# A hybrid convolution-attention block: the convolution's running sum moved to PSUM, the attention scores to shared one-bank halves

## The chip, the cores and the metric

One core of one Trainium2 chip runs the whole kernel. The metric is the device time of one execution in microseconds (us), from the first to the last instruction with the little that lies around them. Engines are named as in the profile: PE is TensorE's matmul, PEld its weight load, DVE VectorE, ACT ScalarE, POOL GpSimd, SP the engine that issues the DMAs. PSUM has eight banks of 512 fp32 values on each of 128 partitions.

## The reference

The input `x` has 2048 rows of 1024 channels. The block is

```
h    = rmsnorm(x)
proj = h @ w_in                       # 7680 columns: glu a, glu b, conv gate, q, k, v, attention gate, two merge gates
c    = silu(layernorm(depthwise_conv31(a * sigmoid(b)) + bias))     # causal, 31 taps, one filter per channel
y_c  = (c * silu(conv_gate)) @ w_conv_out
att  = attention(rope(q), rope(k), v) # 16 query heads, 4 key/value heads, window 128, one sink per head
y_a  = (att * silu(attn_gate)) @ w_attn_out
out  = rmsnorm(x + (sigmoid(m_c) * y_c + sigmoid(m_a) * y_a) @ w_out)
```

Two pieces matter here. The convolution is, for each of 1024 channels, a sum over 31 taps `w[j] * u[t + j - 30]`, then a bias. The attention takes blocks of 128 queries; each block sees its own 128 keys and the 128 before, and the softmax has a sink term beside the scores.

## The kernel before, in words

The 2048 rows are worked in two sweeps of 1024 (`sweep(s)`). In a sweep the channels lie on partitions, in eight chunks of 128, and the rows lie along the free axis, so a tile of the convolution is 128 x 1024. Each product is made from three fp32r matmuls (high times high, high times low, low times high); a projection of 128 columns is two halves of 24 matmuls of 128 x 512, into one of three one-bank tiles of the pool `mm_ps` (line 281).

The order of a sweep is: the projections of k, v and q with rope, interleaved with the eight chunks of the gated unit (`glu_items`), then the four gate projections (`ag`, `cg`, `ma`, `mc`), while convolution and attention run beside them; then the two branch outputs (`ya`, `yc`) and the output product (line 877). In the first sweep the low parts of the weights are made on POOL (`wlo`, line 242) and stored; in the second they are loaded.

PE's order is written out by a planner, the class `Line`. It adds up an estimate of PE's time and inserts steps of other work between groups of three matmuls when their due time has come. Attention on one block of one key/value head is three such steps: the scores (line 566), 22 us later on the planner's clock the transposes of the probabilities (`tpp`, line 594), 16 us later the product with the values (`ov`, line 614). A new block starts each 13.8 us (`ATT_EVERY`), 32 blocks in a sweep. The convolution's taps, one DVE instruction each on 128 x 1024, are handed out every 2.4 us of the planner's clock (`CONV_EVERY`). The other engines' rows are put in order by the compiler's scheduler; each engine then executes its own list strictly in that order and waits at an instruction whose inputs or output buffer are not ready.

The convolution of chunk `c`: the first tap (line 389) multiplies and adds the bias and writes `cv`, a tile in SBUF; 30 more (line 393) each read `glu` at an offset and `cv`, and write `cv`. After the last tap POOL adds `cv` to `csum` for the layer norm.

PSUM's eight banks go to `mm_ps` (three), `tp_ps` (three one-bank tiles, taken in turn) and `sc_ps` (one tile of two banks). All scores of a block, four heads by 256 keys, go to the `sc` tile: ACT copies the older half of the keys to `sb` in SBUF (line 573), DVE lays the block's own keys over it where the mask allows (line 574), and with that both banks are free. From `tp_ps` come `tpp`, which is read by an ACT cast to `pt` (line 599) and a DVE subtraction for its low part (line 242 with `pt<-tpp`), and `ov`, which is read by two ACT copies and two DVE additions (lines 617 and 618). After `pt`, POOL makes `pc`, the part of it that the causal edge lets through (line 605).

Of the kernel before, what the change touches and what calls it, by code (L numbers as in the profile page):

```python
# [12 lines left out]
F32 = mybir.dt.float32  # L13
F32R = mybir.dt.float32r
I32 = mybir.dt.int32
AF = mybir.ActivationFunctionType
ALU = mybir.AluOpType
AX = mybir.AxisListType

P = 128  # L20
# [3 lines left out]
T = 1024  # L24
# [3 lines left out]
TAPS = 31  # L28
# [4 lines left out]
GQ = NH // NKV  # L33
# [20 lines left out]
def hybrid_block(ctx: ExitStack, tc: tile.TileContext, x, par_d, w_in, w_conv, sinks, w_attn, w_out,  # L54
                 fin_g, rope_t, out):
    nc = tc.nc
    pe, act, dve, pool = nc.tensor, nc.scalar, nc.vector, nc.gpsimd
# [4 lines left out]
    work = ctx.enter_context(tc.tile_pool(name="work", bufs=2))  # L62
    mm_ps = ctx.enter_context(tc.tile_pool(name="mm_ps", bufs=3, space=bass.MemoryType.PSUM))
    tp_ps = ctx.enter_context(tc.tile_pool(name="tp_ps", bufs=3, space=bass.MemoryType.PSUM))
    sc_ps = ctx.enter_context(tc.tile_pool(name="sc_ps", bufs=1, space=bass.MemoryType.PSUM))
    dram = ctx.enter_context(tc.tile_pool(name="dram", bufs=1, space=bass.MemoryType.DRAM))

    x2, out2 = x[0], out[0]
# [8 lines left out]
    C = [f"c{i}" for i in range(8)]  # L77
# [3 lines left out]
    def slot(tag, shape, dt, name):  # L81
        n = int(np.prod(shape[1:]))
        full = HALO + T + 2 if tag in WIDE else 1024
        t = slots.tile([P, full], dt, tag=tag, name=name)
        v = t[:, 0:n]
        if len(shape) == 3:
            v = v.rearrange("p (a b) -> p a b", b=shape[2])
        elif len(shape) == 4:
            v = v.rearrange("p (a b c) -> p a b c", b=shape[2], c=shape[3])
        return v  # L90
# [6 lines left out]
    def next_of(key, tags):  # L97
        rot.setdefault(key, cycle(range(len(tags))))
        return tags[next(rot[key])]


    def load_first(half):
        xs = []
        for j in range(4):
# [17 lines left out]
    causal = const.tile([P, P], F32, name="causal")  # L122
    dve.memset(causal, 1.0)
    pool.affine_select(out=causal, in_=causal, pattern=[[-1, P]], compare_op=ALU.is_ge, fill=0.0,
                       base=0, channel_multiplier=1)
    causal_i = causal.bitcast(I32).unsqueeze(1).broadcast_to([P, GQ, P])
    eps = const.tile([P, 2], F32, name="eps_t")
    dve.memset(eps, EPS)
    act.activation(out=eps[:, 1:2], in_=eps[:, 0:1], func=AF.Sqrt)
# [8 lines left out]
    def tap(c, j):  # L138
        return par[:, c, j:j + 1]
# [3 lines left out]
    def cbias(c):  # L143
        return par[:, c, TAPS + 1:TAPS + 2]
# [96 lines left out]
    def split_lo(out_, full, hi, eng):  # L241
        eng.tensor_tensor(out=out_, in0=full, in1=f(hi), op=ALU.subtract)  # L242
# [129 lines left out]
    def sweep(s):  # L372
# [4 lines left out]
            return hT[half][k]  # L377

        glu_slot = [C[7], C[6], AT[14], C[7], C[6], AT[14], C[7], AT[14]]
        glu, cv, conv_done = {}, {}, []  # L380
        csum = work.tile([P, T], F32, tag="ln0", name=f"csum{s}", bufs=1)


        def conv_ops(c):
            ops = []

            def first():
                cv[c] = slot(C[c], [P, T], F32, f"cv{s}_{c}")
                dve.tensor_scalar(out=cv[c], in0=glu[c][:, 0:T], scalar1=tap(c, 0), scalar2=cbias(c),
                                  op0=ALU.mult, op1=ALU.add)  # L390

            def nxt(j):
                dve.scalar_tensor_tensor(out=cv[c], in0=glu[c][:, j:j + T], scalar=tap(c, j),  # L393
                                         in1=cv[c], op0=ALU.mult, op1=ALU.add)
                if j == TAPS - 1:
                    if not conv_done:
                        pool.tensor_copy(out=csum, in_=cv[c])
                    else:
                        pool.tensor_tensor(out=csum, in0=csum, in1=cv[c], op=ALU.add)
                    conv_done.append(c)  # L400
                    if len(conv_done) == KC:
                        line.start(ln_chain())

            ops.append(first)
            for j in range(1, TAPS):
                ops.append(lambda j=j: nxt(j))
            return ops
# [143 lines left out]
        def attention(n):  # L551
            g, b = divmod(n, NB)
            begun.add(n)
            u = f"{s}_{g}_{b}"
            blk = s * NB + b
            first = blk == 0
            q, k = qk.pop(n)
            load_qk(n + 1)
            sc = sc_ps.tile([P, GQ, 2, P], F32, tag="sc", name=f"sc{u}")
            for h in range(GQ):  # L560
                for j in range(2):
                    if first:
                        o, r = sc[:, h, 1, :], k[:, j, P:]
                    else:
                        o, r = sc[:, h], k[:, j]
                    pe.matmul(out=o, lhsT=q[:, h, :], rhs=r, start=(j == 0), stop=(j == 1))  # L566
            ss = slot(next_of("ss", AT[4:7] + AT[13:14]), [P, 1024], F32, f"ss{u}")
            sb = ss[:, 0:512].rearrange("p (h q) -> p h q", q=P)
            oT, ga = (ss[:, c:c + 256].rearrange("p (a q) -> p a q", q=P) for c in (512, 768))
            if first:  # L570
                pool.memset(sb, NEG)
            else:
                act.copy(sb, sc[:, :, 0, :])
            dve.copy_predicated(out=sb, mask=causal_i, data=sc[:, :, 1, :])
            st = work.tile([P, 6, GQ], F32, tag="st", name=f"st{u}", bufs=4)
            mx, ngm, es, den, rinv, dlt = (st[:, i, :] for i in range(6))
            hd = slice(g * GQ, (g + 1) * GQ)
            dve.tensor_reduce(out=mx, in_=sb, axis=AX.X, op=ALU.max, negate=True)
            dve.scalar_tensor_tensor(out=ngm, in0=mx, scalar=SCALE, in1=nsink[:, hd], op0=ALU.mult,  # L579
                                     op1=ALU.min)  # L580
            dve.tensor_tensor(out=dlt, in0=sink_bc[:, hd], in1=ngm, op=ALU.add)
            act.activation(out=es, in_=dlt, func=AF.Exp)
            for h in range(GQ):
                act.activation(out=sb[:, h, :], in_=sb[:, h, :], func=AF.Exp, scale=SCALE,  # L584
                               bias=ngm[:, h:h + 1], accum_out=den[:, h:h + 1])
            dve.tensor_tensor(out=den, in0=den, in1=es, op=ALU.add)
            dve.reciprocal(out=rinv, in_=den)
            for h in range(GQ):
                act.activation(out=sb[:, h, :], in_=sb[:, h, :], func=AF.Copy, scale=rinv[:, h:h + 1])
            yield 0.96, LAT[0]  # L590

            tpp = tp_ps.tile([P, GQ, P], F32, tag="tp", name=f"tpp{u}")
            for h in range(GQ):
                pe.transpose(out=tpp[:, h, :], in_=sb[:, h, :], identity=ident)  # L594
            e2 = slice(s * KC + 2 * g, s * KC + 2 * g + 2)
            qs = slice(b * P, (b + 1) * P)
            nc.sync.dma_start(out=ga, in_=spill["ag"][e2, :, qs].rearrange("c p q -> p c q"))
            pt = slot(next_of("pt", AT[7:9]), [P, 2, GQ, P], F32R, f"pt{u}")
            act.copy(pt[:, 0], tpp)
            split_lo(pt[:, 1], tpp, pt[:, 0], dve)  # L600
            if first:
                seq = [(v_of(g, b), pt)]
            else:
                pc = slot(next_of("pc", AT[9:11]), [P, 2, GQ, P], F32R, f"pc{u}")
                pool.affine_select(out=pc, in_=f(pt), pattern=[[0, 2], [0, GQ], [1, P]],  # L605
                                   compare_op=ALU.is_ge, fill=0.0, base=0, channel_multiplier=-1)
                seq = [(v_of(g, b - 1), pt), (vd[b // 2][:, b % 2, g, :], pc)]
            yield 0.44, LAT[1]

            ov = tp_ps.tile([P, GQ, P], F32, tag="tp", name=f"ov{u}")  # L610
            nm = 2 * len(seq)
            for i in range(nm):
                vv, pp = seq[i // 2]
                pe.matmul(out=ov, lhsT=vv, rhs=pp[:, i % 2], start=(i == 0), stop=(i == nm - 1))  # L614
            ovp = ov.rearrange("p (i r) q -> p i r q", r=2)
            for r, own, other in ((0, slice(0, HD), slice(HD, P)), (1, slice(HD, P), slice(0, HD))):
                act.copy(oT[own], ovp[other, :, r, :])
                dve.tensor_tensor(out=oT[own], in0=ovp[own, :, r, :], in1=oT[own], op=ALU.add)
            dve.tensor_tensor(out=oT, in0=oT, in1=ga, op=ALU.mult)
            hl = sb.rearrange("p (l c) q -> p l c q", c=2)  # L620
            act.copy(hl[:, 0].bitcast(F32R), oT)
            split_lo(hl[:, 1].bitcast(F32R), oT, hl[:, 0], dve)
            for i in range(2):
                nc.sync.dma_start(out=d_a[e2, :, i, qs].rearrange("c p q -> p c q"), in_=hl[:, i])
            done[n] = True
            if n == NKV * NB - 1 and s + 1 < NSWEEP:
                pool.tensor_copy(out=v_halo, in_=f(vt[NB // 2 - 1][:, 1]).rearrange(
                    "p g (a d) -> p g a d", d=HD))
            yield nm * MM_US, 0.0
# [327 lines left out]
```

## Time and profile before

| | |
|---|---|
| runs | 2091.12, 2091.15, 2089.14 us; median 2091.12 |
| profiled execution | span 2089.1 us, as long as the shortest run |
| PE busy | 2046.8 us, 98% of the span |
| PEld, DVE, ACT, POOL busy | 1674.2, 1395.1, 1014.5, 478.3 us |
| mean granted TensorE clock | 0.993 of full |

A row of the profile names line, engine, operation, output and inputs; times in it are us unless marked ns. "Idle before, releaser" is how long an engine stood still before an instruction, and what let it go. PE is pipelined, so its busy share says little about how fast it runs: its waits and its granted clock say more.

### The profile page before, as it was taken

To read this page: it belongs to the slowest core of one execution; us is meant where nothing else is said; L and a number is where in the kernel's file an instruction comes from. 1 tells how busy PE (TensorE), PEld (TensorE's weight loads), DVE (VectorE), ACT (ScalarE), POOL (GpSimd) and SP (SyncE) were. 2 spreads that over 40 slices of the span, in tenths; PEclk is the share of its full clock that TensorE was granted. 3 is DMA by queue.
4 is the path that set the end of the run, shared out by engine and by line. 5 is a ranking of instruction groups with operands and counts; after the bars stand their busy time and mean duration, and the time that the engine had idled before them with its cause. 6 is when DMAs were issued, how large, how long until landed. Compare 5 with 4: busy or idle time off the path is not lost.

```text
span 2089.1 us, 27438 instructions
## 1 busy us (share of the span) xinstructions
PE 2046.8 (98%) x9256; PEld 1674.2 (80%) x9256; DVE 1395.1 (67%) x1901; ACT 1014.5 (49%) x2253; POOL 478.3 (23%) x336
## 2 busy tenths in 40 slices
PE   7999999999999999999999999999999999999998
PEld 6787888787787878888888888888888888888887
DVE  4979779899888348123559596698888934341324
ACT  6221376665666646122442214767777674621222
POOL 2445433343333322243001131121111110000200
PEclk9999999999999999999999999999999999999999
DMA  7444645554445875646344456555655577574432
GB/s 250 134 143 149 191 148 154 165 158 148 152 146 178 262 238 190 203 141 222 101 151 132 141 162 202 173 158 175 174 163 165 174 228 257 166 232 146 139 120 81
DMA packets 265819, 355.89 MB, mean 170 GB/s; under 512 B 28112, under 2 KB 126544, under 8 KB 265680
## 3 DMA queue, kind: packets, MB, share of 16 engines
q1 hardware_dynamic: 265680, 354.16, 53.2%
q8 instruction: 73, 1.20, 0.2%
q14 instruction: 66, 0.54, 0.1%
HBM read 234.51 MB, written 119.54 MB: 169 GB/s over the span
## 4 chain that ended last, share of the span: by engine, by line
PE 80%; DVE 5%; issue 2%; ACT 1%; DMA 0%; POOL 0%; SPq 0%; DVEq 0%; ACTq 0%; POOLq 0%
PE mm_ag L281 9%; PE o L877 8%; PE mm_mc L281 8%; PE mm_yc L281 8%; PE mm_ya L281 8%; PE mm_cg L281 7%; PE mm_gb L281 6%; PE mm_ma L281 6%; PE mm_ga L281 6%; DVE cv L393 3%; PE mm_q_b L281 2%; PE sc L566 2%; PE ov L614 2%; PE mm_q_a L281 2%; PE tpp L594 1%
## 5 line engine op out<-in xcount | busy, mean ns | idle before, releaser
L393 DVE SCALAR_TENSOR_TENSOR cv<-glu,par,cv 128x1024 f32<-128x1024 f32 x480 | 680.5, 1418 | 6.2
L605 POOL TENSOR_SCALAR_AFFINE_SELECT pc<-pt 128x1024 fp32r<-128x1024 f32 x60 | 101.9, 1698 | 458.0 <-DVE pt L242 390.4
L877 PE MATMUL o<-wo,mT 128*128 128x512 f32 x768 | 181.3, 394 | 0.0
L281 PE MATMUL mm_cg<-hT,whi_cg 128*128 128x512 f32 x512 | 164.2, 402 | 5.2 <-ACT glu L415 3.3
L877 PEld LDWEIGHTS o<-wo,mT 128*128 128x128 f32 x768 | 143.1, 188 | 32.1
L281 PE MATMUL mm_ga<-hT,whi_ga 128*128 128x512 f32 x512 | 162.4, 398 | 3.0 <-ACT ag L434 2.8
L281 PE MATMUL mm_ma<-hT,whi_ma 128*128 128x512 f32 x512 | 161.2, 396 | 1.0 <-ACT ma L434 1.0
L281 PE MATMUL mm_ag<-hT,whi_ag 128*128 128x512 f32 x512 | 160.9, 395 | 1.2 <-ACT glu L415 1.2
L281 PE MATMUL mm_gb<-hT,whi_gb 128*128 128x512 f32 x512 | 161.9, 398 | 0.0
L281 PE MATMUL mm_mc<-hT,whi_mc 128*128 128x512 f32 x512 | 159.8, 393 | 0.0
L281 PE MATMUL mm_yc<-uT,whi_yc 128*128 128x512 f32 x512 | 159.4, 392 | 0.0
L281 PE MATMUL mm_ya<-aT,whi_ya 128*128 128x512 f32 x512 | 158.7, 391 | 0.0
L281 PEld LDWEIGHTS mm_cg<-hT,whi_cg 128*128 128x128 f32 x512 | 95.8, 192 | 25.9 <-ACT glu L415 3.7
L281 PEld LDWEIGHTS mm_ga<-hT,whi_ga 128*128 128x128 f32 x512 | 95.1, 190 | 24.4 <-ACT ag L434 3.2
L281 PEld LDWEIGHTS mm_yc<-uT,whi_yc 128*128 128x128 f32 x512 | 96.2, 188 | 21.8
L281 PEld LDWEIGHTS mm_mc<-hT,whi_mc 128*128 128x128 f32 x512 | 96.0, 188 | 21.9 <-ACT mc L434 0.2
L281 PEld LDWEIGHTS mm_ya<-aT,whi_ya 128*128 128x128 f32 x512 | 96.1, 188 | 21.0
L281 PEld LDWEIGHTS mm_gb<-hT,whi_gb 128*128 128x128 f32 x512 | 95.5, 190 | 20.2
L281 PEld LDWEIGHTS mm_ag<-hT,whi_ag 128*128 128x128 f32 x512 | 94.2, 188 | 21.1 <-ACT glu L415 1.7
L281 PEld LDWEIGHTS mm_ma<-hT,whi_ma 128*128 128x128 f32 x512 | 94.0, 188 | 20.9 <-ACT ma L434 1.8
L584 ACT ACTIVATE ss<-ss,st 128x128 f32<-128x128 f32 x256 | 99.8, 391 | 20.2 <-DVE st L579 19.5
L815 POOL TENSOR_TENSOR lmc<-lmc,mp 128x512 f32<-128x512 f32 x32 | 41.9, 1310 | 275.5 <-DVE lmc L814 271.2
(363 smaller groups left out, 4338.6 us busy)
## 6 DMA issues: line engine op xcount, KB each, us to landing
qk<-d_q SPq DMA_DIRECT2D x256, 64.0 KB, 2.6
d_a<-ss SPq DMA_DIRECT2D x128, 128.0 KB, 1.9
aT<-d_a SPq DMA_DIRECT2D x32, 512.0 KB, 6.1
qk<-d_k SPq DMA_DIRECT2D x240, 64.0 KB, 2.1
raw_gb<-in_w_in_dram SPq DMA_DIRECT2D x34, 256.0 KB, 3.8
raw_ga<-in_w_in_dram SPq DMA_DIRECT2D x34, 256.0 KB, 3.4
raw_ag<-in_w_in_dram SPq DMA_DIRECT2D x32, 256.0 KB, 3.8
d_ag<-ag SPq DMA_DIRECT2D x32, 256.0 KB, 2.2
```

The source lines that it names most:

```text
L281: pe.matmul(out=ps, lhsT=a, rhs=b, start=(k == 0 and i == 0), stop=(k == KC - 1 and i == 2))
L393: dve.scalar_tensor_tensor(out=cv[c], in0=glu[c][:, j:j + T], scalar=tap(c, j), in1=cv[c], op0=ALU.mult, op1=ALU.add)
L566: pe.matmul(out=o, lhsT=q[:, h, :], rhs=r, start=(j == 0), stop=(j == 1))
L584: act.activation(out=sb[:, h, :], in_=sb[:, h, :], func=AF.Exp, scale=SCALE, bias=ngm[:, h:h + 1], accum_out=den[:, h:h + 1])
L594: pe.transpose(out=tpp[:, h, :], in_=sb[:, h, :], identity=ident)
L605: pool.affine_select(out=pc, in_=f(pt), pattern=[[0, 2], [0, GQ], [1, P]], compare_op=ALU.is_ge, fill=0.0, base=0, channel_multiplier=-1)
L614: pe.matmul(out=ov, lhsT=vv, rhs=pp[:, i % 2], start=(i == 0), stop=(i == nm - 1))
L815: pool.tensor_tensor(out=g, in0=g, in1=mp[e][:, half * TH:(half + 1) * TH], op=ALU.add)
L877: pe.matmul(out=ps, lhsT=a[:, c0:c0 + P], rhs=r, start=(k == 0 and i == 0), stop=(k == KC - 1 and i == 2))
```

## The change

The pool `sc_ps` is gone, and its two banks become `cv_ps`, one tile of 128 x 1024 fp32 for the convolution's running sum (`acc`). The first tap writes `acc`, the next 29 read and write it, and the last reads `acc` and writes `cv` in SBUF, which is only taken then. The scores now come in two tiles of one bank each, two heads in each, from `tp_ps`, so that a block takes four tiles in turn from its three banks: two for scores, one for `tpp`, one for `ov`. ACT's copy and DVE's masked copy are made once for each half.

```
-    sc_ps = ctx.enter_context(tc.tile_pool(name="sc_ps", bufs=1, space=bass.MemoryType.PSUM))
+    cv_ps = ctx.enter_context(tc.tile_pool(name="cv_ps", bufs=1, space=bass.MemoryType.PSUM))
...
             def first():
-                cv[c] = slot(C[c], [P, T], F32, f"cv{s}_{c}")
-                dve.tensor_scalar(out=cv[c], in0=glu[c][:, 0:T], scalar1=tap(c, 0), scalar2=cbias(c),
+                acc[c] = cv_ps.tile([P, T], F32, tag="acc", name=f"acc{s}_{c}")
+                dve.tensor_scalar(out=acc[c], in0=glu[c][:, 0:T], scalar1=tap(c, 0), scalar2=cbias(c),
                                   op0=ALU.mult, op1=ALU.add)
             def nxt(j):
-                dve.scalar_tensor_tensor(out=cv[c], in0=glu[c][:, j:j + T], scalar=tap(c, j),
-                                         in1=cv[c], op0=ALU.mult, op1=ALU.add)
+                to = acc[c]
+                if j == TAPS - 1:
+                    to = cv[c] = slot(C[c], [P, T], F32, f"cv{s}_{c}")
+                dve.scalar_tensor_tensor(out=to, in0=glu[c][:, j:j + T], scalar=tap(c, j),
+                                         in1=acc[c], op0=ALU.mult, op1=ALU.add)
...
-            sc = sc_ps.tile([P, GQ, 2, P], F32, tag="sc", name=f"sc{u}")
+            scs = []
             for h in range(GQ):
+                if h % 2 == 0:
+                    scs.append(tp_ps.tile([P, 2, 2, P], F32, tag="tp", name=f"sc{u}_{h // 2}"))
+                sc = scs[-1][:, h % 2]
...
-            else:
-                act.copy(sb, sc[:, :, 0, :])
-            dve.copy_predicated(out=sb, mask=causal_i, data=sc[:, :, 1, :])
+            for i, sc in enumerate(scs):
+                part = sb[:, 2 * i:2 * i + 2, :]
+                if not first:
+                    act.copy(part, sc[:, :, 0, :])
+                dve.copy_predicated(out=part, mask=causal_i, data=sc[:, :, 1, :])
```

PE's order stays as it was, save that the eight score matmuls of a block now go to two tiles. The names in the rows are those of the code with the sweep left out: `sc_0_4` is the scores of head group 0, block 4. Here is PE's list in the first sweep, at the end of one projection half, before the change:

```order
L281 MATMUL mm_gb_30_2355<-hT_0_7_131,whi_gb_31_2216 128x512 x2
L281 MATMUL mm_gb_30_2355<-hT_0_7_131,wlo_gb_31_2217 128x512
L614 MATMUL ov_0_1_2396<-pt_0_1_2237,vt_0_759 128x512 x2
L614 MATMUL ov_0_1_2396<-pc_0_1_2240,vd_0_760 128x512 x2
L566 MATMUL sc_0_4_2420<-qk_4_2268 128x256 x8
L281 MATMUL mm_gb_31_2447<-hT_1_0_313,whi_gb_30_2210 128x512 x2
```

And the same place now:

```order
L281 MATMUL mm_gb_30_2368<-hT_0_7_131,whi_gb_31_2226 128x512 x2
L281 MATMUL mm_gb_30_2368<-hT_0_7_131,wlo_gb_31_2227 128x512
L622 MATMUL ov_0_1_2409<-pt_0_1_2247,vt_0_759 128x512 x2
L622 MATMUL ov_0_1_2409<-pc_0_1_2250,vd_0_760 128x512 x2
L572 MATMUL sc_0_4_0_2433<-qk_4_2278 128x256 x4
L572 MATMUL sc_0_4_1_2438<-qk_4_2278 128x256 x4
L281 MATMUL mm_gb_31_2463<-hT_1_0_313,whi_gb_30_2220 128x512 x2
```

Nothing moved here, but the bank behind `sc_0_4_1` is now the one that `tpp_0_2` had, whose transposes stand eleven rows further up in the same list.

DVE's list keeps its order in the main, with a tap more or less at many places. Here it is in the second sweep, around the subtraction that frees the bank of `tpp_0_4`, before the change:

```order
L586 TENSOR_TENSOR st_0_5_11488<-st_0_5_11488 128x4
L389 TENSOR_SCALAR cv_3_11647<-glu_3_11319,par 128x1024
L587 RECIPROCAL st_0_5_11488<-st_0_5_11488 128x4
L393 SCALAR_TENSOR_TENSOR cv_3_11647<-glu_3_11319,par,cv_3_11647 128x1024 x3
L242 TENSOR_TENSOR pt_0_4_11567<-tpp_0_4_11561,pt_0_4_11567 128x512
L393 SCALAR_TENSOR_TENSOR cv_3_11647<-glu_3_11319,par,cv_3_11647 128x1024 x2
L618 TENSOR_TENSOR ss_0_3_11214<-ov_0_3_11589,ss_0_3_11214 64x256
L393 SCALAR_TENSOR_TENSOR cv_3_11647<-glu_3_11319,par,cv_3_11647 128x1024
L618 TENSOR_TENSOR ss_0_3_11214<-ov_0_3_11589,ss_0_3_11214 64x256
L574 COPY_PREDICATED ss_0_6_11623<-causal,sc_0_6_11614 128x512
```

And the same place now:

```order
L594 TENSOR_TENSOR st_0_5_11608<-st_0_5_11608 128x4
L389 TENSOR_SCALAR acc_3_11771<-glu_3_11433,par 128x1024
L595 RECIPROCAL st_0_5_11608<-st_0_5_11608 128x4
L396 SCALAR_TENSOR_TENSOR acc_3_11771<-glu_3_11433,par,acc_3_11771 128x1024 x2
L242 TENSOR_TENSOR pt_0_4_11687<-tpp_0_4_11681,pt_0_4_11687 128x512
L396 SCALAR_TENSOR_TENSOR acc_3_11771<-glu_3_11433,par,acc_3_11771 128x1024 x3
L626 TENSOR_TENSOR ss_0_3_11326<-ov_0_3_11709,ss_0_3_11326 64x256
L582 COPY_PREDICATED ss_0_6_11745<-causal,sc_0_6_0_11735 128x256
L582 COPY_PREDICATED ss_0_6_11745<-causal,sc_0_6_1_11740 128x256
L626 TENSOR_TENSOR ss_0_3_11326<-ov_0_3_11709,ss_0_3_11326 64x256
```

Here one tap moved behind the subtraction on `pt`, and the masked copy became two. Over all blocks of a sweep, between a block's row maximum and the next subtraction on `pt`, 118 and 114 taps stand now in the two sweeps, where 120 and 115 stood.

More of the change, by code (lines that the diff above doesn't have):

```diff
@@ L125, in hybrid_block @@
                        base=0, channel_multiplier=1)
-    causal_i = causal.bitcast(I32).unsqueeze(1).broadcast_to([P, GQ, P])
+    causal_i = causal.bitcast(I32).unsqueeze(1).broadcast_to([P, 2, P])
     eps = const.tile([P, 2], F32, name="eps_t")
@@ L379, in sweep @@
         glu_slot = [C[7], C[6], AT[14], C[7], C[6], AT[14], C[7], AT[14]]
-        glu, cv, conv_done = {}, {}, []
+        glu, cv, acc, conv_done = {}, {}, {}, []
         csum = work.tile([P, T], F32, tag="ln0", name=f"csum{s}", bufs=1)
@@ L558, in attention @@
             load_qk(n + 1)
-            sc = sc_ps.tile([P, GQ, 2, P], F32, tag="sc", name=f"sc{u}")
+            scs = []
             for h in range(GQ):
+                if h % 2 == 0:
+                    scs.append(tp_ps.tile([P, 2, 2, P], F32, tag="tp", name=f"sc{u}_{h // 2}"))
+                sc = scs[-1][:, h % 2]
                 for j in range(2):
                     if first:
-                        o, r = sc[:, h, 1, :], k[:, j, P:]
+                        o, r = sc[:, 1, :], k[:, j, P:]
                     else:
-                        o, r = sc[:, h], k[:, j]
+                        o, r = sc, k[:, j]
                     pe.matmul(out=o, lhsT=q[:, h, :], rhs=r, start=(j == 0), stop=(j == 1))
```

## The prediction, as put on record

> **What bounds the kernel now.** The page's first part comes first: one engine is busy nearly all the time.
>
> ```profile
> PE 2046.8 (98%) x9256; PEld 1674.2 (80%) x9256; DVE 1395.1 (67%) x1901; ACT 1014.5 (49%) x2253; POOL 478.3 (23%) x336
> ```
>
> So only two things can move the end: what PE waits for, and the clock that it is granted. PE's own waits from 60 us on, in the order of their size (those under 1 us are left out, here and in the sums):
>
> ```profile
> PE mm_q_b L281 <- DVE rb_q__1_1524 L467: 3.4, 1, 3.4
> PE mm_cg L281 <- ACT glu L415: 3.3, 1, 3.3
> PE mm_gb L281 <- POOL wlo_gb L242: 3.0, 1, 3.0
> PE mm_ga L281 <- ACT ag L434: 2.8, 1, 2.8
> PE tpv L499 <- ACT vs L519: 2.2, 1, 2.2
> PE mm_cg L281 <- ACT cg L434: 1.9, 1, 1.9
> PE sc L566 <- issue: 1.4, 1, 1.4
> PE mm_q_b L281 <- DVE ra_q__0_1408 L461: 1.3, 1, 1.3
> PE mm_ag L281 <- ACT glu L415: 1.2, 1, 1.2
> PE mm_ma L281 <- ACT ma L434: 1.0, 1, 1.0
> ```
>
> They sum to 21.5 us, and all lie in the first sweep: the second has none. Most are a bank of `mm_ps` that ACT or DVE has not emptied in time. The granted clock shows that a wait can cost more than its length. Six gaps are of 1.9 us or more, and each is followed by a window at half clock; here are the first, the longest and the last of these six windows, then, for contrast, the stretch behind a gap of 1.2 us (the granted clock is the third figure from the end), and the rows of PE's timeline for one gap of each kind.
>
> ```profile
> 95.30:98.50 3.20, 3.20 (x9) 2.52 (x8) 3.20 (x8) 1.98 (x7) 0.18 (x1) 0.50 0.00 0
> 525.40:532.00 6.60, 5.67 (x15) 4.55 (x16) 3.73 (x9) 5.07 (x12) 2.14 (x2) 0.50 0.48 158
> 576.60:579.80 3.20, 3.20 (x10) 2.56 (x9) 3.20 (x6) 1.99 (x3) 0.39 (x1) 0.50 0.17 48
> 386.00:396.00 10.00, 10.00 (x48) 8.19 (x47) 8.70 (x15) 7.55 (x18) 2.92 (x3) 1.00 0.53 157
> ```
>
> ```profile
> 200.15 0.70 PE L281 MATMUL mm_q_b<-hT,whi_q_b 128*128 128x512 f32 x2 [3.42 <-DVE rb_q__1_1524 L467]
> 384.82 0.73 PE L281 MATMUL mm_ag<-hT,whi_ag 128*128 128x512 f32 x2 [1.23 <-ACT glu L415]
> ```
>
> With the edges that these rows leave off, five windows are some 3.4 us long and one is twice that: seven times 3.4 us at half speed lose 7 x 1.7 = 11.9 us. The first sweep therefore loses 21.5 + 11.9 = 33.4 us that the second does not.
>
> Why only the first? These rows compare two like stretches in the attention stage, one of each sweep: all engines (PE, PEld, DVE, ACT, POOL, clock), then the taps alone on DVE.
>
> ```profile
> 350.00:650.00 300.00, 285.65 (x1310) 232.65 (x1309) 275.86 (x352) 195.09 (x465) 108.63 (x71) 0.97 0.51 155
> 1350.00:1650.00 300.00, 300.00 (x1428) 248.62 (x1427) 271.82 (x383) 213.14 (x512) 48.92 (x27) 1.00 0.56 168
> ```
>
> ```profile
> 350.00:650.00 300.00, 184.45 (x127) 0.97 0.51 155
> 1350.00:1650.00 300.00, 185.38 (x137) 1.00 0.56 168
> ```
>
> A tap takes 184.45 / 127 = 1.452 us in the first sweep and 185.38 / 137 = 1.353 in the second, and POOL is busy 108.6 against 48.9 us. DVE's work against PE's is 275.86 / 285.65 = 96.6% in the first sweep, 271.82 / 300 = 90.6% in the second. DVE falls behind in the first, and ACT with it, since they take turns on each block. DVE is not the bound, but it sets when PSUM banks come free.
>
> **The change part by part.** First the taps. By their operands the rows are minimum/median/maximum in ns:
>
> ```profile
> L393 DVE SCALAR_TENSOR_TENSOR cv<-glu,par,cv x480: 1254/1285/2394, 53.8 to 1670.6; 128x1024 f32<-128x1024 f32 x160
> L389 DVE TENSOR_SCALAR cv<-glu,par x16: 801/814/1616, 52.3 to 1619.4; 128x1024 f32<-128x1024 f32 x16
> ```
>
> ```profile
> L242 DVE TENSOR_TENSOR hl_k<-ra_k,hl_k x8: 693/1676/1786, 68.0 to 1126.0; 128x512 fp32r<-128x512 f32 x8
> ```
>
> ```profile
> L711 DVE TENSOR_TENSOR lcg<-lcg,cv x32: 677/691/694, 803.0 to 1847.1; 128x512 f32<-128x512 f32 x32
> ```
>
> ```profile
> L419 DVE TENSOR_TENSOR glu<-mm_ga,glu x32: 660/691/693, 33.6 to 1618.2; 128x512 f32<-128x512 f32 x32
> ```
>
> Two inputs from SBUF cost 691 ns where POOL leaves them alone and up to 1786 where it does not. One input from PSUM and one from SBUF (`glu<-mm_ga,glu`) costs 691 in the median and 693 at most, in a stage where POOL is at work. So I take a tap with its sum in PSUM at the undisturbed 1.285 us. What the trace does not show is a DVE write to PSUM, nor a read and a write of one bank by one instruction. The bounds: 1.254, the least of any tap, and 1.353, a tap of the second sweep (the rivals go beyond). I take 1.285, as the two 691s say that PSUM costs nothing on the read side.
>
> [...]
>
> The first tap is a multiply-add on one tensor at 814 ns for 1024 elements, less than a tap. With PSUM as its output I bound it by 0.81 and 1.285 us and take the upper end, as it writes where the taps write: +0.47 us, four times in such a stretch, 1.9 us. [...]
>
> Now the halves. Full and half size on DVE and ACT (the `ov` rows have 256 elements, the score rows 512):
>
> ```profile
> L574 DVE COPY_PREDICATED ss<-causal,sc x64: 717/741/760, 238.8 to 1711.5; 128x512 f32<-128x512 int32 x64
> L573 ACT COPY ss<-sc x60: 577/587/590, 251.7 to 1710.8; 128x512 f32<-128x512 f32 x60
> ```
>
> ```profile
> L618 DVE TENSOR_TENSOR ss<-ov,ss x128: 403/422/429, 284.4 to 1754.8; 64x256 f32<-64x256 f32 x128
> L617 ACT COPY ss<-ov x128: 363/368/372, 284.0 to 1753.5; 64x256 f32<-64x256 f32 x128
> ```
>
> On DVE 256 elements less save 691 - 422 = 269 ns, so half a masked copy takes 741 - 269 = 472 and the pair 203 ns more. On ACT two copies of 368 are 149 ns more than one of 587. With 300 / 13.8 = 21.7 blocks in such a stretch DVE gains 21.7 x 0.203 = 4.4 us of work, ACT 3.2 us; ACT at 213 of 300 us has room, and its share is inside the uncertainty below. PE's matmuls are the same.
>
> DVE's load becomes, in the first sweep, 275.9 - 127 x (1.452 - 1.285) + 4.4 + 1.9 = 261.0 us on 285.65 of PE's, or 91.4%; in the second, 271.8 - 137 x (1.353 - 1.285) + 6.3 = 268.8 of 300, or 89.6%. Both stand near the 90.6% at which the second sweep runs today without one wait. So I expect the old waits to go, and with them the half clocks: 33.4 us, less the `tpv` gap, which lies before the attention and is ended by ACT (2.2 + 1.7 = 3.9), less half of the `wlo_gb` gap, which is ended by POOL ((3.0 + 1.7) / 2 = 2.4). That is 27.1 us.
>
> Third, the added wait. The four tiles of a block go round three banks, so the second score half takes the bank of the `tpp` that PE filled some 4 us earlier (in the last two blocks below the scores come 4.2 and 3.5 us behind the end of the transposes, and their second half 0.55 later). That bank is free when DVE's subtraction on `pt` is through. If it is not, PE stands, and everything behind it: the next projection's matmuls have banks of their own but stand in the same list, and ACT's copy of that half, with ACT's whole queue, waits for PE. In the trace of before, the subtraction and the scores that would wait for it, for three blocks (DVE's rows, then PE's: the transposes of the last two, then the scores of all three):
>
> ```profile
> 265.93 0.68 DVE L242 TENSOR_TENSOR pt<-tpp,pt 128x512 fp32r<-128x512 f32 x1
> 1402.31 0.68 DVE L242 TENSOR_TENSOR pt<-tpp,pt 128x512 fp32r<-128x512 f32 x1
> 1682.74 0.69 DVE L242 TENSOR_TENSOR pt<-tpp,pt 128x512 fp32r<-128x512 f32 x1 [3.17 <-ACT pt L599]
> ```
>
> ```profile
> 1397.37 0.60 PE L594 MATMUL tpp<-ident_r,ss 128*128 128x128 f32 x4
> 1677.31 0.60 PE L594 MATMUL tpp<-ident_r,ss 128*128 128x128 f32 x4
> ...
> 264.32 1.11 PE L566 MATMUL sc<-qk 128*128 128x256 f32 x8
> 1402.20 1.10 PE L566 MATMUL sc<-qk 128*128 128x256 f32 x8
> 1681.44 1.11 PE L566 MATMUL sc<-qk 128*128 128x256 f32 x8
> ```
>
> In the second sweep the subtraction ends after the second half's start in 10 of 30 such pairs, by 0.24 us in the first of them (1402.99 against 1402.75) to 1.44 in the last (1683.43 against 1681.99), 7.75 us together; with 0.1 us for each signal, 8.75. In the first sweep it ends too late in all 30, by 1.74 us in the first: with DVE as late as today this change would only move PE's waits to the scores. So the new wait depends on DVE's load: 8.75 us in a sweep at 90.6%, and at 96.6% what PE pays now, 33.4. That is 4.1 us for each point. At 91.4% the first sweep pays 12.0 us, at 89.6% the second 4.7: 16.7 us, in waits that are mostly too short to halve the clock. The other three tiles of a block take banks that were filled more than twice as long before, and I count no wait for them.
>
> The sum on the profiled execution: 2089.1 - 27.1 + 16.7 = 2078.7 us. The median of the runs is 2.0 us above that execution's time, so I predict 2080.7, rounded to 2081. The last stages have no PE wait to win and keep their time.
>
> **The rivals.** First, gain and wait cancel. The waits at the scores cluster in some blocks instead of being spread; if six of them pass 1.9 us, six windows of half clock add 10.2, and 2078.7 + 10.2 + 2.0 = 2090.9, the median of today. For it: blocks with six taps ahead of the subtraction are where today's second sweep comes late. Against it: none there exceeds 1.44 us.
>
> Second, slower: writing and reading PSUM costs a tap what POOL's company costs it today, and it takes 1.353 us. Then the first sweep has 275.9 - 12.6 + 6.3 = 269.6 us on 285.65, 94.4%, and a wait of 8.75 + 3.8 x 4.1 = 24.3 us; the second 278.1 of 300, 92.7%, and 17.4. The sum is 2089.1 - 27.1 + 41.7 + 2.0 = 2105.7. For it: no row writes PSUM from DVE. Against it: the equal medians of 691. Between 16.7 us of waits at 1.285 and 41.7 at 1.353, the 27.1 won are used up at a tap of 1.313 us; from there the change is a loss.
>
> Third, much slower: the change doesn't shed what it is meant to shed. If reading and writing one bank takes turns, 1024 elements cost another 1.07 us (269 ns for 256), a tap 2.35; DVE then has 271.8 + 6.3 + 137 x 1.0 = 415 us of work in 300 of PE's, 38% too much over some 870 us of attention: 330 us more, about 2420. No row speaks for it.
>
> **How the numbers follow.** Forecast 0.56, cancel 0.22, PSUM tap slower 0.17, much slower 0.05. About 0.2% of the time, 4.2 us, is what a measurement can tell from no change. So: faster 0.56, within 0.2% 0.22, slower 0.22. The forecast's own range is 2066 to 2087: at the low end all 33.4 us go and 8.3 us of waits come, at the high end the new waits reach 23 us. The range that should hold the time goes up to the second rival: 2066 to 2106.
>
> **What would show it.** Right: taps at one length near 1.285 us in both sweeps; no gap from 100 to 700 us at `mm` tiles; six half-clock windows reduced to one or two; small gaps at the scores (line 572) that are ended by DVE's `pt`, 10 to 20 us in all, in both sweeps. Wrong: taps above 1.31 us; scores waiting over 27 us in total; gaps at `mm` tiles that stay although DVE's load fell, which would mean that ACT or POOL, not DVE, emptied the banks late.

## The result, and the profile after

The changed kernel takes 2053.02 us (median of four runs, 2052.67 to 2053.49) against 2090.43 (four runs, 2089.14 to 2091.15): a ratio of 0.982, 95% interval 0.981 to 0.984. The sign was forecast, the size was not: 37 us were won where 10 were expected, and the result lies 13 us below the low end of the range. Ratios, here and below, leave out three executions in a slower state, one of e6 and two of the kernel before.

The page's first part, and the row of its span, for the kernel after:

```profile
span 2051.5 us, 27562 instructions
PE 2031.3 (99%) x9256; PEld 1669.1 (81%) x9256; DVE 1327.4 (65%) x1965; ACT 1027.8 (50%) x2313; POOL 403.4 (20%) x336
```

The row of its core and granted clock (0.993 before):

```profile
core 0: 2051.5 us, clock 0.999
```

PE ran the same 9256 matmuls. No window at half clock is left before the last matmul, where there were six. DVE issued 64 instructions more and was still busy for 68 us less, and so was POOL, by 75 us, although no line of POOL's work was changed. The shares of the chain that ended last, before and then after:

```profile
PE 80%; DVE 5%; issue 2%; ACT 1%; DMA 0%; POOL 0%; SPq 0%; DVEq 0%; ACTq 0%; POOLq 0%
```

```profile
PE 96%; DVE 2%; DMA 1%; issue 0%; SPq 0%; POOL 0%; ACT 0%; DVEq 0%; POOLq 0%
```

PE's list of waits is now this, complete (line, tile, what ended the wait, us in total, times, longest):

```profile
PE tpf L361 <- DVE ident_r L117: 8.4, 1, 8.4
PE tpf L361 <- DVE xf L354: 2.4, 2, 1.5
PE sc L572 <- DVE pt L242: 1.0, 1, 1.0
PE mm_ga L281 <- POOL wlo_ga L242: 0.7, 1, 0.7
PE tpf L361 <- DVE hT L364: 0.5, 1, 0.5
PE mm_ga L281 <- ACT whi_ga L253: 0.2, 1, 0.2
```

All but the third belong to the first 60 us, which the change doesn't touch. Of the ten waits that the prediction added up, none is left, nor is any of the smaller ones (1.9 us in all) beside them. The wait that the change was to add, the scores for the bank of `tpp`, is there once, with 1.0 us. Here it is in PE's timeline: the transposes, the products before the scores, then the two halves of the scores; and DVE's rows beside it.

```profile
346.20 0.60 PE L602 MATMUL tpp<-ident_r,ss 128*128 128x128 f32 x4
...
349.90 0.63 PE L622 MATMUL ov<-pc,vd 128*128 128x512 f32 x2
350.37 0.64 PE L572 MATMUL sc<-qk 128*128 128x256 f32 x4
351.97 0.74 PE L572 MATMUL sc<-qk 128*128 128x256 f32 x4 [0.97 <-DVE pt L242]
```

```profile
347.39 3.94 DVE L396 SCALAR_TENSOR_TENSOR acc<-glu,par,acc 128x1024 f32<-128x1024 f32 x3
351.24 0.68 DVE L242 TENSOR_TENSOR pt<-tpp,pt 128x512 fp32r<-128x512 f32 x1
```

Three taps in a row stood ahead of the subtraction, it ended 5.1 us behind the transposes, and the second half could only start then. So the mechanism of this wait is the one that the prediction described, but it happens in one block of 64.

The taps and the first tap of the kernel after (minimum/median/maximum in ns), then POOL's `pc`, before and after:

```profile
L396 DVE SCALAR_TENSOR_TENSOR acc<-glu,par,acc x464: 1257/1290/1291, 53.9 to 1634.6; 128x1024 f32<-128x1024 f32 x155
L389 DVE TENSOR_SCALAR acc<-glu,par x16: 1334/1347/1349, 52.5 to 1581.1; 128x1024 f32<-128x1024 f32 x16
```

```profile
L605 POOL TENSOR_SCALAR_AFFINE_SELECT pc<-pt x60: 1089/2072/2463, 284.5 to 1735.6; 128x1024 fp32r<-128x1024 f32 x60
```

```profile
L613 POOL TENSOR_SCALAR_AFFINE_SELECT pc<-pt x60: 1087/1094/1107, 266.0 to 1697.7; 128x1024 fp32r<-128x1024 f32 x60
```

The longest tap went from 2394 to 1291 ns: nothing stretches a tap any more. And the taps no longer stretch POOL: `pc`, the same instruction on the same data, went from a median of 2072 to 1094 ns. The two engines had been slowing each other: with both inputs of a tap in SBUF by up to 1.1 us on a tap and 1.0 us in the median on `pc`, and hardly at all once the tap took one of them from PSUM (1291 and 1107 ns at most).

**Where the time went.** PE's list has the same matmuls in the same order in both kernels, so each can be paired with itself and its start compared. Worked out so from the two traces, the kernel after stands 0.3 us behind at 92 us of the kernel before and leads by 37.9 us at 781, a gain of 38.2 in steps at the old gaps (a lead of 2.1 at `tpv`, 5.2 to 11.3 at the `mm_q_b` gaps, 20.0 by 487 us, 33 by 576); it stays at 37.9 through the whole second sweep, and 0.3 us go again behind the last matmul. Of the 38.2 us, 21.5 are the waits of the prediction's list, 1.9 the smaller ones, 11.9 the half-clock windows by the prediction's count (the starts themselves show 10.9), less 1.0 for the new wait; 3.9 are left. Most of these lie in how a gap is counted: it starts at the end of the matmul before, but in PE's rows a matmul that doesn't wait starts 0.16 us ahead of that end (350.37 above, against 349.90 + 0.63). Each of the 16 old gaps moved the lead by 0.15 to 0.17 us more than its row says, 2.6 us in all. The last 1.3 us (2.3 with the 10.9) have no cause that was found.

### The profile page after: what moved, and what is told of

The parts are those of the page before. It is cut to its first block, busy times and chain, and to the rows that moved or that the text cites. A ratio compares the mean times of both kernels' runs of the same rounds, so it can differ in the third digit from the quotient of the medians.

```text
span 2051.5 us, 27562 instructions
## 1 busy us (share of the span) xinstructions
PE 2031.3 (99%) x9256; PEld 1669.1 (81%) x9256; DVE 1327.4 (65%) x1965; ACT 1027.8 (50%) x2313; POOL 403.4 (20%) x336
## 4 chain that ended last, share of the span: by engine, by line
PE 96%; DVE 2%; DMA 1%; issue 0%; SPq 0%; POOL 0%; ACT 0%; DVEq 0%; POOLq 0%
PE mm_cg L281 9%; PE o L885 9%; PE mm_ma L281 9%; PE mm_ga L281 9%; PE mm_mc L281 9%; PE mm_yc L281 9%; PE mm_ya L281 9%; PE mm_gb L281 8%; PE mm_ag L281 7%; PE mm_q_a L281 4%; PE mm_q_b L281 4%; PE sc L572 3%; PE ov L622 3%; PE mm_v L281 2%; DVE acc L396 2%; PE tpp L602 1%
## 5 line engine op out<-in xcount | busy, mean ns | idle before, releaser
L396 DVE SCALAR_TENSOR_TENSOR acc<-glu,par,acc 128x1024 f32<-128x1024 f32 x464 | 596.3, 1285 | 6.2
L613 POOL TENSOR_SCALAR_AFFINE_SELECT pc<-pt 128x1024 fp32r<-128x1024 f32 x60 | 65.6, 1094 | 428.7 <-DVE pt L242 428.6
L281 PE MATMUL mm_ga<-hT,wlo_ga 128*128 128x512 f32 x256 | 100.8, 394 | 0.7 <-POOL wlo_ga L242 0.7
```

The lines of the kernel that those rows point to most:

```text
L281: pe.matmul(out=ps, lhsT=a, rhs=b, start=(k == 0 and i == 0), stop=(k == KC - 1 and i == 2))
L396: dve.scalar_tensor_tensor(out=to, in0=glu[c][:, j:j + T], scalar=tap(c, j), in1=acc[c], op0=ALU.mult, op1=ALU.add)
```

## The experiments

Each kernel ran on the chip beside the kernel before, which took 2089.4 to 2090.4 us in the median of these sets; all ratios are to it. One number is worked out for each kernel from the records of its trace: the *distance*, from the end of the transposes of `tpp` to the end of DVE's subtraction on `pt`, the mean over 30 blocks of a sweep (the first and the last left out) and, in brackets, the longest of them. In the kernel after the second score half comes 3.5 to 5.0 us behind the transposes, 4.7 in the median, so a longer distance means a wait there when the halves share the banks.

| kernel | median us, ratio (95%) | distance, first sweep | second sweep |
|---|---|---|---|
| before | 2090.4 | 11.5 (18.1) | 3.7 (5.7) |
| after | 2053.0, 0.982 (0.981 to 0.984) | 2.8 (5.1) | 2.3 (3.8) |
| e1 halves, three banks | 2109.9, 1.010 (1.008 to 1.011) | 4.5 (10.5) | 3.4 (5.5) |
| e2 halves, five banks | 2092.0, 1.001 (1.000 to 1.002) | 10.9 (14.5) | 4.4 (7.2) |
| e8 POOL quiet | 2051.7, 0.982 (0.980 to 0.983) | 3.1 (5.4) | 2.4 (3.9) |
| e10 `wlo` quiet | 2051.4, 0.982 (0.980 to 0.983) | 4.8 (8.7) | 3.8 (5.8) |
| e11 `pc` quiet | 2081.1, 0.996 (0.995 to 0.998) | 10.9 (17.4) | 2.6 (4.8) |
| e9 sum in PSUM, no halves | 2077.0, 0.994 (0.992 to 0.995) | 3.0 (5.9) | 2.1 (3.5) |
| e3 memset for every second tap | 2052.9, 0.982 (0.981 to 0.984) | 2.7 (5.1) | 2.3 (3.8) |
| e4 memset for each tap | 2056.1, 0.984 (0.982 to 0.986) | 2.9 (5.9) | 2.3 (3.8) |
| e5 small copy behind every second tap | 2054.0, 0.983 (0.981 to 0.984) | 2.7 (5.9) | 2.3 (3.5) |
| e6 small copy behind each tap | 2052.8, 0.982 (0.980 to 0.984) | 2.9 (4.9) | 2.4 (4.2) |
| e7 wide copy behind each tap | 2057.3, 0.984 (0.983 to 0.986) | 3.0 (6.1) | 2.3 (3.7) |
| e12 small copy, sum in SBUF | 2129.6, 1.019 (1.017 to 1.021) | 12.3 (17.0) | 9.8 (15.3) |

The theories, which the recorded expectations call by letters: company (A, and C in the last run), POOL reading SBUF made DVE late, and the taps got rid of it, while the halves only pay for the banks; halves (B), these bring a part by themselves, as they free the score banks sooner; load (L), it is DVE's busy share as such, as the prediction's rule had it.

**The halves alone (e1, e2).** The kernel before with the change's second half only: scores in one-bank halves from `tp_ps`, the convolution in SBUF. In e1 `tp_ps` keeps three banks and two stand idle; in e2 it has all five.

```
-    sc_ps = ctx.enter_context(tc.tile_pool(name="sc_ps", bufs=1, space=bass.MemoryType.PSUM))
...
-            sc = sc_ps.tile([P, GQ, 2, P], F32, tag="sc", name=f"sc{u}")
+            scs = []
             for h in range(GQ):
+                if h % 2 == 0:
+                    scs.append(tp_ps.tile([P, 2, 2, P], F32, tag="tp", name=f"sc{u}_{h // 2}"))
```

> The score halves on the three shared banks, the running sum left in SBUF (two banks idle). Theory A (company): what made the first sweep late is POOL stretching taps whose two inputs are both in SBUF, so a tap stays at 1.42 us on the mean, DVE stays about 11 us late in the first sweep, and PE now waits at the scores for the subtraction on pt in most of its 30 blocks: 2095 to 2125 us, scores waiting over 20 us. Theory B (halves): the finer steps of the scores shorten the chain by themselves, the first sweep's waits shrink without any help from PSUM: under 2075 us.

> As the run before, but the transposes' pool has five banks, so that no score waits for a transpose. Theory A: the halves are worth nothing, 2085 to 2100 us, with the old gaps at the projections' banks in the first sweep and none in the second, where the subtraction on pt still ends 3 to 4 us behind the transposes. Theory B: under 2070 us, and that distance falls to 2.3 us in the second sweep as in the changed kernel.

e1 took 2109.94 us, e2 2091.96 (the median of the kernel before beside them was 2089.94). In e1, PE's waits and the groups row of the taps (busy us, mean ns):

```profile
PE sc L568 <- DVE pt L241: 32.2, 20, 6.9
```

```profile
L392 DVE SCALAR_TENSOR_TENSOR cv<-glu,par,cv 128x1024 f32<-128x1024 f32 x480 | 676.5, 1409 | 6.3
```

With the taps stretched (1409 ns in the mean), the wait that the prediction feared is there, in 20 blocks and with 32.2 us (27.8 of them in 14 blocks of the first sweep), and the halves cost 20 us. With two banks more it is gone, and the old gaps are back, for instance:

```profile
PE mm_q_b L280 <- DVE rb_q__1_1521 L466: 3.4, 1, 3.4
PE mm_ma L280 <- ACT ma L433: 3.3, 2, 2.1
PE mm_ga L280 <- ACT whi_ga L252: 3.3, 1, 3.3
PE mm_ag L280 <- ACT glu L414: 3.1, 1, 3.1
```

So the halves are worth nothing by themselves, and theory B falls.

**The company alone (e8, e10, e11).** The kernel before with its sum in SBUF and its two-bank score tile, but with POOL writing zeros in place of reading SBUF: the low parts of the weights in e10, `pc` in e11, both in e8, save one column of each. These kernels leave out that part of the computation. The order of DVE's list can't explain what they gain: in e11 it is that of the kernel before, and in e8 and e10 1891 of 1901 rows stand in that order, the others being a memset at the start and nine rows behind the attention of the first sweep.

```
-                split_lo(lo, raw, hi, pool)
+                pool.memset(f(lo), 0.0)
+                split_lo(lo[:, :, 0:1], raw[:, :, 0:1], hi[:, :, 0:1], pool)
...
-                pool.affine_select(out=pc, in_=f(pt), pattern=[[0, 2], [0, GQ], [1, P]],
+                pool.memset(f(pc), 0.0)
+                pool.affine_select(out=pc[:, :, :, 0:1], in_=f(pt)[:, :, :, 0:1], pattern=[[0, 2], [0, GQ], [1, 1]],
```

> The kernel before, in which POOL no longer reads SBUF at length: the low parts of the weights (first sweep) and the causal part of the probabilities are set to zero, save one column each that is computed as before, so that order and waits stay. It leaves that part of the computation out. DVE's list is that of the kernel before. Theory A (company): taps fall to 1.29 us without any PSUM and the time to 2053 to 2062 us. Rival (place): the running sum in PSUM matters for itself, and this kernel stays above 2075 us.

> The kernel before with POOL's low parts of the weights set to zero save one column (left out of the computation), the causal part as it was. POOL's company in the first sweep is then that of the second, whose distance between transposes and the end of the subtraction was 3.7 us without a wait. Theory A: the first sweep's distance falls from 11.5 to under 5 us and its gaps go: 2051 to 2060 us.

> The other half: the causal part of the probabilities set to zero save one column (left out), the low parts of the weights as they were. Theory A: the second sweep's taps fall to 1.29 us and its distance from 3.7 to about 2.4 us, with no effect on the time there; the first sweep keeps the company of the weights' low parts, its distance falls part of the way: 2060 to 2085 us.

e8 took 2051.67 us, as little as the kernel after, and its PE waits for nothing past the start. The groups rows of the taps, in the kernel before, in e11, e10 and e8:

```profile
L393 DVE SCALAR_TENSOR_TENSOR cv<-glu,par,cv 128x1024 f32<-128x1024 f32 x480 | 680.5, 1418 | 6.2
```

```profile
L393 DVE SCALAR_TENSOR_TENSOR cv<-glu,par,cv 128x1024 f32<-128x1024 f32 x480 | 663.1, 1381 | 6.2
```

```profile
L394 DVE SCALAR_TENSOR_TENSOR cv<-glu,par,cv 128x1024 f32<-128x1024 f32 x480 | 644.7, 1343 | 6.2
```

```profile
L394 DVE SCALAR_TENSOR_TENSOR cv<-glu,par,cv 128x1024 f32<-128x1024 f32 x480 | 623.6, 1299 | 6.2
```

The whole gain is had without moving the sum, by removing what read SBUF beside it. The weights' low parts (`wlo`) do nearly all of it: without them e10 takes 2051.37 us, 38 less than the kernel before in its set, and its `pc` is as stretched as before:

```profile
L606 POOL TENSOR_SCALAR_AFFINE_SELECT pc<-pt x60: 1088/2072/2464, 267.2 to 1696.0; 128x1024 fp32r<-128x1024 f32 x60
```

In e10 POOL also has less to do (528 ns of memset for a `wlo_gb` that took 1436 in the median), so alone it doesn't tell a late DVE from a late POOL; but in the kernel after POOL does its full work, and the gaps are gone as well.

Without `pc` alone e11 takes 2081.12 us, 8 less than the kernel before in its set, and the gaps stay:

```profile
PE mm_q_b L281 <- DVE rb_q__1_1524 L467: 3.4, 1, 3.4
PE mm_cg L281 <- ACT glu L415: 3.3, 1, 3.3
PE mm_gb L281 <- POOL wlo_gb L242: 2.6, 1, 2.6
```

`pc` matters elsewhere: for the distance. Without it the second sweep's goes from 3.7 to 2.6 us. That is the number on which the prediction's price for the halves was built, and so that price held the company of `pc`, which the change also removes. DVE's load in that stretch fell as well, from 90.6% to 88.5%:

```profile
1350.00:1650.00 300.00, 300.00 (x1429) 248.75 (x1428) 265.61 (x392) 214.56 (x508) 50.46 (x50) 1.00 0.57 169
```

So e11 doesn't tell company from load in the second sweep. The runs e5 to e7 below do, with another order of DVE's list.

**The sum alone (e9).** The other half of the change: `acc` in PSUM as in the kernel after, the two-bank score tile kept, and the two banks taken from `mm_ps` and `tp_ps` (two each).

```
-    mm_ps = ctx.enter_context(tc.tile_pool(name="mm_ps", bufs=3, space=bass.MemoryType.PSUM))
-    tp_ps = ctx.enter_context(tc.tile_pool(name="tp_ps", bufs=3, space=bass.MemoryType.PSUM))
+    mm_ps = ctx.enter_context(tc.tile_pool(name="mm_ps", bufs=2, space=bass.MemoryType.PSUM))
+    tp_ps = ctx.enter_context(tc.tile_pool(name="tp_ps", bufs=2, space=bass.MemoryType.PSUM))
+    cv_ps = ctx.enter_context(tc.tile_pool(name="cv_ps", bufs=1, space=bass.MemoryType.PSUM))
```

> The running sum in PSUM alone: the scores keep their two-bank tile, and the sum's two banks are taken one each from the projections' pool (two left) and the transposes' pool (two left). Theory A: with taps at 1.29 us DVE is punctual, a projection's bank is emptied within the 5.5 us of the other half, and the score halves were not needed: 2052 to 2062 us. Rival: two banks are too few for the projections when ACT stands 2 to 3 us behind: over 2070 us, with gaps at the projections' tiles.

2077.03 us (2072.14 to 2078.61). The taps are the same as after (1285 ns in the mean), but PE waits again, mostly for ACT to empty the projections' banks (the profile is of the shortest of the four executions):

```profile
PE mm_mc L282 <- ACT mc L438: 4.9, 3, 2.5
PE mm_ga L282 <- ACT glu L419: 3.5, 1, 3.5
PE lnvar L662 <- ACT rstd L704: 2.1, 2, 1.2
PE mm_ya L282 <- DVE mp L795: 1.8, 1, 1.8
```

So the halves earn 24 us (2077.0 against 2053.0) as the cheaper way to pay for two banks.

**Load without company (e3 to e7).** The kernel after with DVE work added behind the taps, to test the prediction's 4.1 us for each point of load. e3 and e4 add a memset of 32 columns behind every second and every tap:

```
+                if j % 2 == 0:
+                    dve.memset(scr, 0.0)
```

> The changed kernel with a tiny DVE instruction behind every second tap, some 0.06 us on each tap in the mean, as much as the second rival of the prediction put on it. By the prediction's own rule (4.1 us of waits for each point of DVE load) this costs 2.9 points in each sweep, 24 us: 2077 us, and more at 4.1 us a point if the instruction is dearer. By theory A, in which the scores wait only where the subtraction ends over 4.5 us behind the transposes, six taps add 0.4 us to distances of 2 to 5 us: 2053 to 2058 us.

> The same with the tiny instruction behind every tap, some 0.12 us each, which makes a tap nearly as long as it was in the first sweep before. By the prediction's rule 48 us: about 2101 us. By theory A six taps add 0.7 us to the distances, of which five in the first sweep and one in the second then pass the limit by 4 us in all: 2055 to 2067 us. A rival: it is the mean length of the taps that matters and nothing else, then the first sweep falls behind as it did before the change, and the time goes back to 2085 us or more.

2052.89 us and 2056.10 (ratios 0.982 and 0.984), but they missed their aim: the memset depends on nothing, and the compiler's scheduler put all 480 of them, 85 ns each, into the first 294 us in e4, mostly ahead of the taps that they were to follow; e4's scores wait 3.3 us in two blocks. So a copy that depends on the tap, of 32 columns behind every second tap (e5), every tap (e6), and of 256 columns (e7):

```
+                if j < TAPS - 1:
+                    dve.tensor_copy(out=scr, in_=acc[c][:, 0:32])
```

> The two runs before this one missed their aim: their tiny instruction depended on nothing and was put ahead of the taps. Here it is a copy of 32 columns of the running sum behind every second tap, which the next tap has to wait for: an estimated 0.07 us on each tap in the mean, the second rival's price. The prediction's rule (4.1 us of waits for each point of DVE load) gives 24 us: about 2077 us. Theory A (PE waits only where the subtraction on pt ends over 4.5 us behind the transposes) adds 0.4 us to distances of 2 to 5 us: 2053 to 2060 us.

> The same behind every tap, an estimated 0.14 us on each, which brings a tap to 1.43 us, nearly the 1.45 of the first sweep before. The prediction's rule: about 2101 us. Theory A: distances grow by 0.8 us, a few blocks pass the limit, 2056 to 2070 us, with no gap at the projections' banks. Rival: the mean length of a tap is all that matters, and the first sweep is late again: 2085 us or more.

> The same with 256 columns, an estimated 0.4 us on each tap. DVE then has more work than PE in the attention stage (262 + 125 x 0.4 = 312 us in a stretch of 300), and both theories see PE wait at the scores: 2100 to 2170 us, in both sweeps alike. It marks the far end of the curve.

2053.97, 2052.83 and 2057.30 us. The copies in e7 are work indeed, and here are its waits at the scores, all that there are:

```profile
L401 DVE COPY scr<-acc 128x256 f32<-128x256 f32 x464 | 195.1, 420 | 7.2
```

```profile
PE sc L576 <- DVE pt L244: 3.0, 2, 1.9
```

These are the stretches of the three kernels after, e6 and e7 in which PE has about the work that it had in the prediction's two windows (earlier by the lead), all engines:

```profile
341.00:614.00 273.00, 272.03 (x1296) 225.54 (x1295) 250.72 (x371) 196.64 (x483) 82.03 (x70) 1.00 0.54 170
1312.00:1612.00 300.00, 300.00 (x1427) 248.77 (x1426) 266.33 (x405) 218.57 (x537) 32.88 (x27) 1.00 0.55 169
```

```profile
341.00:614.00 273.00, 272.58 (x1297) 225.81 (x1296) 263.76 (x490) 195.26 (x484) 81.87 (x69) 1.00 0.56 170
1312.00:1612.00 300.00, 300.00 (x1428) 248.66 (x1427) 279.59 (x529) 215.31 (x534) 32.91 (x27) 1.00 0.58 170
```

```profile
341.00:614.00 273.00, 271.90 (x1294) 225.08 (x1293) 263.87 (x453) 193.45 (x481) 82.22 (x70) 1.00 0.55 168
1312.00:1612.00 300.00, 300.00 (x1430) 248.76 (x1429) 281.97 (x499) 209.62 (x525) 32.57 (x29) 1.00 0.57 168
```

DVE's load on PE's time is 92.2% and 88.8% after, 96.8% and 93.2% in e6, 97.0% and 94.0% in e7. By the prediction's rule e6 would pay 34 and 19 us at the scores; it pays 0.4 and nothing. e7 would pay 35 and 23; it pays 3.0 and nothing. Both theories had expected more of e7 than came. Part of it is that the compiler knows of the copies: it moved taps back (the last one ends 60 us later than in the kernel after) and spread them more evenly. Between a block's row maximum and the next subtraction on `pt` e7 has 130 and 129 taps in its two sweeps, more than the 118 and 114 of the kernel after, but never more than five in one block, where that has up to seven. For contrast, e10's row for the first of these stretches, with `pc` still stretched:

```profile
341.00:614.00 273.00, 273.00 (x1301) 226.34 (x1300) 245.85 (x350) 192.08 (x459) 82.32 (x112) 1.00 0.54 167
```

Its load is 90.1%, the least of the four kernels, and its distance in that sweep the longest of them (4.8 us against 2.8 to 3.0). So load that the order allows for, on an engine that nothing disturbs, cost little here up to 97%: e7 is 4 us slower than the kernel after.

**The same load with company (e12).** The kernel before, with a copy of 32 columns of `cv` behind every tap, in SBUF.

```
+                if j < TAPS - 1:
+                    dve.tensor_copy(out=scr, in_=cv[c][:, 0:32])
```

> The kernel before with one more DVE instruction behind every tap, a copy of 32 columns of the running sum in SBUF (0.1 to 0.19 us), which the scheduler knows of when it makes DVE's list. Theory C (plan): DVE falls behind by time that its list was not made for, that is by POOL's company, and not by its load; then 15 to 25 us more work in each sweep cost little: 2085 to 2100 us. Theory L (load, the prediction's rule): the first sweep's load goes from 96.6% to over 100% of PE's time: 2110 us or more.

2129.59 us, 40 us more than the kernel before, where e6 with the same copy on the kernel after cost nothing. The copy in e12, and a stretch of its second sweep:

```profile
L398 DVE COPY scr<-cv 128x32 f32<-128x32 f32 x464 | 124.7, 269 | 7.7
```

```profile
1385.00:1685.00 300.00, 294.60 (x1391) 241.00 (x1390) 282.92 (x489) 197.41 (x479) 35.97 (x27) 1.00 0.53 161
```

A load of 96.0% goes with a distance of 9.8 us here, one of 97.0% in e7's first sweep with 3.0. The number that came is the one which L had named for e12, and company's, 2100 at most, missed. But L can't tell this run from e7, nor e6 from e10: the busy share alone doesn't say how late DVE is. Company and added work were worse together in this run than either theory has it; the copies themselves are stretched too, 269 ns in the mean where the shortest take 152. What stays open is why. It may be that the order of DVE's list is made for the undisturbed durations, so that what stretches a row in the middle has no place to be made up; no run here had such unplanned slowness without POOL, and this was not shown. e12's list also has another order than that of the kernel before, so even a comparison of these two holds more than the copies.

No run points to a version that beats the kernel after by more than can be measured: only 1.0 us of its waits past the start lies at the scores, and e8 and e10, with none, are 1.4 and 1.7 us faster while they leave work out.

## Why the prediction was wrong in size

Some rows more are needed: of the kernel after, the groups row of the masked half (busy us, mean ns); and of the kernel before, what DVE and ACT did ahead of the `tpv` gap.

```profile
L582 DVE COPY_PREDICATED ss<-causal,sc 128x256 f32<-128x256 int32 x128 | 54.9, 445 | 6.2 <-ACT ss L581 3.9
```

```profile
79.26 12.34 DVE L393 SCALAR_TENSOR_TENSOR cv<-glu,par,cv 128x1024 f32<-128x1024 f32 x8
91.52 0.55 DVE L502 TENSOR_TENSOR vd<-tpv,vf 128x384 f32<-128x384 f32 x1
```

```profile
92.10 0.41 ACT L513 CAST vd<-vd 128x256 fp32r<-128x256 f32 x1 [10.62 <-DVE vd L502]
```

- **The taps: right.** 1.285 us was forecast; the median is 1.290, in both sweeps and with no long ones. For a tap, reading and writing the sum in PSUM cost hardly more than in SBUF (1290 against 1285 ns). The two rivals of a slow PSUM tap, at 1.353 and 2.35 us, fall with that.
- **The first tap: a little over its bound**, 1.347 us against the 1.285 taken. Before, with its output in SBUF, it took 0.814 us; that a multiply-add writing PSUM takes 533 ns more is measured, why it does was not shown. Sixteen times 62 ns more are 1.0 us of DVE's time, and no wait shows it.
- **The halves on DVE: cheaper.** A masked half was estimated at 472 ns and takes 445 in the mean (row above), so a pair costs 149 ns more than the 741 of the whole, not 203.
- **DVE's load: right.** 91.4% and 89.6% were forecast, 92.2% and 88.8% came for the same work of PE, with 126 and 137 taps in the two stretches.
- **The old waits: too little taken.** 27.1 of 33.4 us were to go, and all went. The `tpv` gap (2.2 us, ended by ACT) and the `wlo_gb` gap (3.0, ended by POOL) were held to be other engines' doing. e1, e2 and e11, where the taps are still stretched by `wlo`, keep the `tpv` gap with 2.1 to 2.2 us; the kernel after, e8, e9 and e10 have none. The engine that ends a wait isn't always the one that is late. Ahead of the `tpv` gap, in the kernel before, ACT had itself stood 10.6 us for DVE, which was at eight taps in a row of 1.54 us each (rows above; in the kernel after seven stand there, at 1.32). POOL was held up by the taps directly: its `wlo_gb` that ended the gap there took 2.23 us, as against 1.30 in the median of the kernel after. All of the 33.4 us is 6.3 more than was taken; with 1.9 us of gaps under 1 us, which the sum left out, and 3.9 around the gaps, this part is 12.1 us.
- **The step that failed: the new wait at the scores**, "4.1 us for each point" of DVE's load. It was forecast at 16.7 us and is 1.0: 15.7 us. The rule drew a line through two points, a sweep with little company and one with much, and gave the difference to the load. But both points held company: the second sweep's distance of 3.7 us falls to 2.6 when `pc` is quiet (e11), and at like loads (90.1% in e10's first sweep, 92.2% after) the distance is 4.8 and 2.8, though with another order of DVE's list. The prediction named the cause of the lateness in its first part, POOL beside the taps, and then priced the new wait as if only its effect on the busy time counted. With the company left in, in e1, the scores do wait, 27.8 us in the first sweep and 4.4 in the second, where the rule's two points were 33.4 (half clock included) and 8.75. Without it, e6 and e7 carry loads for which the rule asks 53 and 58 us, and pay 0.4 and 3.0. (The 0.1 us that the rule added for each signal is 0.05 in the one wait that came: the subtraction ends at 351.92, the scores start at 351.97.)
- **The cancel rival** needed six waits of 1.9 us at the scores; there was one of 1.0.

The two errors point the same way: 15.7 + 12.1, less 0.6 (0.3 us longer after at the start and 0.3 at the end), make the 27.2 us between the forecast span of 2078.7 and the measured 2051.5.

## What to carry to other kernels

When the same instruction shows a maximum far above its median (2394 ns against 1285 here), find out who stretches it before counting load: here the engine beside it was stretched too (`pc`, 2072 ns against 1094), and taking one operand to PSUM freed both. Price a new wait from a stretch that lacks the disturbance which the change removes, not from the one that has it; and a bank that has to be given up is best taken from the tile whose reader is punctual (halves of the scores here: 24 us better than a bank each from two pools). A wait is put down to the engine that ended it, and that engine may only be passing on another's delay, as ACT did at the `tpv` gap, where it had itself stood 10.6 us for DVE.

## What the runs showed of the hardware

- POOL reading SBUF beside a tap with two SBUF inputs cost both: up to 1.1 us on a tap of 1.285, and 1.0 us in the median on a `pc` of 1.09. With POOL writing zeros for `wlo`, save one column, the kernel took 38 us less, 1.8% of its time (e10), although POOL was busy for only 23% of the span.
- The accumulation that reads and writes the same two PSUM banks ran at 1290 ns in the median for 1024 elements, within 5 ns of the 1285 of that in SBUF; the multiply-add with PSUM output took 1347 where it had taken 814 with its output in SBUF.
- A gap of PE cost about 0.16 us more than its row shows (0.15 to 0.17 at each of the 16 old gaps). In the kernel before, the six gaps of 1.9 us and more each cost some 1.6 us more in the half-clock window of 3.4 us behind it, or 2.8 in the double one: a row of 2.2 us stood for 4. Length alone didn't decide it: the gap of 3.5 us in e9 had no such window (the clock from 350 to 650 us is 1.00 there), and of the five gaps of 2.1 to 3.4 us in e11 at most three had one, an estimate from its mean clock of 0.997 and the 1.7 us that a window loses.
